# Attention: four of twelve turns of the probabilities go from TensorE to GpSimd and transposing transfers, and stand elsewhere in the written order

## The chip, the cores and the metric

The kernel runs on one core of one Trainium2 chip. The metric is the device time of one execution in microseconds (us). Before the change three runs took 966.99, 967.45 and 968.06 us; the median is 967.45 us. The profile is one further execution.

## What is computed

A trunk of two layers over 256 positions with 1024 features, all in float32: a gated linear recurrence, then attention, each between two half-step SwiGLU blocks. The change touches only the attention, which the reference computes for two query blocks of 128 positions:

```python
q = (xq @ w_q).reshape(Bn, S, N_HEADS, HEAD_DIM).transpose(0, 2, 1, 3) * (HEAD_DIM ** -0.5)
for blk in range(S // Q_BLOCK):
    q0 = blk * Q_BLOCK
    end = q0 + Q_BLOCK
    logits = jnp.einsum('bhqd,bhkd->bhqk', q[:, :, q0:end], k[:, :, :end]).astype(jnp.float32)
    logits = logits + c[:, :, q0:end, None] - c[:, :, None, :end]
    ...
    p = jax.nn.softmax(logits, axis=-1).astype(v.dtype)
    outs.append(jnp.einsum('bhqk,bhkd->bhqd', p, v[:, :, :end]))
o = jnp.concatenate(outs, axis=2).transpose(0, 2, 1, 3).reshape(Bn, S, D_ATTN)
return o @ w_o
```

There are 16 heads of 64 features. The first query block (the first half, `t == 0`) sees 128 keys, the second (`t == 1`) 256.

## The kernel before, in words

Every large product is made of three passes over split operands: a weight tile `raw` (512 KB, loaded by a transfer on SP's queue) is split into an upper part `whi` (ScalarE, L173) and a lower part `wlo` (VectorE, L177, which subtracts one SBUF tensor from another), and activations are split likewise (`xhi` and `xlo`, or `oh` and `ol` behind the attention). TensorE then runs upper by upper, upper by lower and lower by upper into one bank. Five `raw` buffers and nine pairs of parts stand between the loads and TensorE.

In the attention a group is four heads of the first half (groups 0 to 3) or two of the second (groups 0 to 7), that is 128 by 512 probabilities each. Four steps make a group:

- `logits` (l): TensorE multiplies queries and keys for two groups at once into two `gt` banks (L1138). VectorE adds the bias row by row and finds the maximum (L1147: `gt` in PSUM, bias in SBUF), adds and subtracts `cq` in two tiny tensor_tensor operations on `mx` (L1151, L1152; 128 by 4 or by 2 elements, all in SBUF), and ScalarE takes the exponentials and their sums (L1154).
- `norm` (n): VectorE inverts the sums (L1160) and multiplies the group by them (L1161, both inputs in SBUF).
- `turn` (t): TensorE transposes the group in four pieces of 128 by 128 into a `tr` bank (L1167), and ScalarE copies it to a `pT` tile (L1169).
- `values` (v): TensorE multiplies `pT` and the values (L1181). Behind two groups of the first half, or four of the second, ScalarE and VectorE split the result into `oh` and `ol` (L1187, L1188).

TensorE's program order is written out by hand. In the attention it is the string `ATT_ORDER`: a digit is half a weight unit (eight units of the query projection, L428 to L432, then eight of the output projection, L183 to L185, each once for either half of the positions), and a letter with a digit is the next step of that kind and that half. A letter l for an odd group does nothing, since the even one before it made both. Heads of the queries are turned two ticks after their projection is done (L1001, from a tile `htok` that VectorE writes at L996). The other engines' instructions, and the transfers, are put in order by the framework from priorities and due times, and then stand fixed in each engine's queue. Each queue runs in order.

The feed-forward blocks already turn their hidden activations without TensorE: GpSimd copies the tile into two planes of 16-bit halves (L527), SP issues a transposing transfer of the planes (L535), and GpSimd joins the halves again (L540). The keys take the same way through the helpers `planes`, `swap` and `join` (L212, L216, L220, or L1016).

Of the kernel before, what the change touches and what calls it, by code (L numbers as in the profile page):

```python
# [9 lines left out]
F32 = mybir.dt.float32  # L10
F32R = mybir.dt.float32r
BF16 = mybir.dt.bfloat16
U16 = mybir.dt.uint16
# [4 lines left out]
P = 128  # L18
# [25 lines left out]
def trunk_kernel(ctx: ExitStack, tc: tile.TileContext, A: dict, out: bass.AP):  # L44
# [6 lines left out]
    hpool = ctx.enter_context(tc.tile_pool(name="h", bufs=1))  # L51
# [6 lines left out]
    def nm(s):  # L58
        uid[0] += 1
        return f"{s}_{uid[0]}"  # L60
# [7 lines left out]
    def trbank():  # L68
        return psum.tile([P, 512], F32, tag="tr", name=nm("tr"), bufs=2)
# [36 lines left out]
    h = [hpool.tile([P, D], F32, tag=f"h{t}", name=f"h{t}") for t in range(2)]  # L106
# [103 lines left out]
    def planes(dst, src):  # L210

        nc.gpsimd.tensor_copy(dst.rearrange("p (h f) -> p h f", h=2), src.bitcast(U16).rearrange("p (f h) -> p h f", h=2))  # L212

    def swap(turned, halves):

        tc.keep_in_program_order(nc.sync.dma_start(turned.rearrange("p (a b) -> p a b", b=P), halves, transpose=True))  # L216

    def join(dst, turned):

        nc.gpsimd.tensor_copy(dst, turned.rearrange("p (h f) -> p h f", h=2))  # L220
# [895 lines left out]
    def attention(t):  # L1116

        ap = pools["a"]
# [4 lines left out]
        box = {}  # L1123
# [37 lines left out]
            nc.vector.tensor_tensor(pe, pe, sm.unsqueeze(2).to_broadcast([P, per, nk * P]), ALU.mult)  # L1161

        def turn(hg):
            tp = trbank()
            pev = box["pe", hg].rearrange("p a b -> p (a b)")
            for j in range(4):
                nc.tensor.transpose(tp[:, j * P:(j + 1) * P], pev[:, j * P:(j + 1) * P], ident)  # L1167
            pT = box["pT", hg] = ap.tile([P, 4, P], F32, tag="pT", name=nm("pT"), bufs=4)
            nc.scalar.activation(pT.rearrange("p a b -> p (a b)"), tp, AF.Copy)  # L1169

        def values(hg):

            hds = range(hg * per, (hg + 1) * per)
            if hds[0] % 8 == 0:
                box["po"] = mmbank()
            po, pT = box["po"].rearrange("p (a b) -> p a b", a=4), box["pT", hg]
            for j in range(0, per, 2):
                for k in range(nk):
                    for s in range(2):
                        hd = hds[j + s]  # L1180
                        nc.tensor.matmul(po[s * HD:(s + 1) * HD, hd % 8 // 2, :], kv["v"][k][:, hd * HD:(hd + 1) * HD],  # L1181
                                         pT[:, (j + s) * nk + k, :], start=k == 0, stop=k == nk - 1)
            if hds[-1] % 8 == 7:
                b = hds[-1] // 8
                oh_v = att["oh"][t][:, 4 * b:4 * b + 4, :].rearrange("p a b -> p (a b)")
                ol_v = att["ol"][t][:, 4 * b:4 * b + 4, :].rearrange("p a b -> p (a b)")
                nc.scalar.activation(oh_v, box["po"], AF.Copy)  # L1187
                nc.vector.tensor_tensor(ol_v, box["po"], oh_v.bitcast(F32), ALU.subtract)  # L1188

        return {c: [lambda i=i, f=f: f(i) for i in range(G)] for c, f in zip("lntv", (logits, norm, turn, values))}  # L1190

    def post_q(n):
        return lambda t, ps: heads_T(ps, t, n, HD ** -0.5, att["q"][t])

    for n in range(2):
# [9 lines left out]
    ffn_items(lambda: pools["f"], A["ffn2_w_gate"][1], A["ffn2_w_up"][1], A["ffn2_w_down"][1], A["ffn2_post_g"][1],  # L1205
              lambda t: None, last=True)

    ATT_ORDER = ("0 0 0 0 0 0 0 l0 0 1 n0 l0 1 1 t0 n0 1 l0 v0 1 t0 n0 l0 1 v0 n0 1 t0 l1 1 v0 t0 n1 l1 0 v0 "
                 "n1 l1 t1 0 n1 l1 t1 0 n1 l1 v1 v1 t1 0 n1 l1 t1 0 n1 l1 v1 v1 t1 0 n1 l1 t1 0 n1 v1 v1 0 t1 1 "
                 "t1 v1 1 v1 1 1 1 1 1 1")  # L1210


    def half(t, i):
# [178 lines left out]
    att_rows()  # L1392

    steps = [attention(0), attention(1)]
    nxt = [n_ffn3, n_ffn3]
    for c in ATT_ORDER.split():
        if c[0] in "lntv":
# [45 lines left out]
```

## Time and profile before

| | before |
|---|---|
| median of three runs | 967.45 us |
| the profiled execution | 967.64 us |
| its span in the trace | 965.9 us, so 1.7 us lie around it |
| TensorE busy | 957.7 us of the span |
| granted TensorE clock over the span | 0.998 |
| attention steps on TensorE | from 721.18 us (first logits) to 769.1 us (start of the last values) |

The chain of waits follows the work that ended last backwards from the end; it names the engine that sets the time. The list of waits says for how long an engine stood idle and what ended that. The timeline shows single instructions with their start and duration. Matmuls are pipelined, so that their durations overlap: what one costs is the distance from its start to the next start. A busy share close to one says little here; the absence of idle time in front of TensorE's instructions says more.

### The profile page before, as it was taken

The numbers are of one execution on the slowest core, as the hardware profiler recorded it, in microseconds if no ns is written. First come the engines' busy times: TensorE is split into PE (matmuls) and PEld (weight loads), VectorE is DVE, ScalarE is ACT, GpSimd is POOL, SyncE is SP. The second block draws the span as 40 slices with busy tenths as digits, with TensorE's granted clock in tenths as the row PEclk, the third lists the DMA queues.
The fourth block names the chain that finished last, engine by engine and source line by source line (L and its number), as shares of the span: only waits on it lengthen the run. The fifth ranks groups of instructions, "written<-read, shape, count | busy, mean of one in ns | idle before, by whom it ended". The sixth has DMA issues, their size and how long they took to land.

```text
span 965.9 us, 12879 instructions
## 1 busy us (share of the span) xinstructions
PE 957.7 (99%) x4591; PEld 793.3 (82%) x4591; DVE 637.2 (66%) x845; ACT 528.9 (55%) x753; POOL 207.1 (21%) x211
## 2 busy tenths in 40 slices
PE   9999999999999999999999999999999999999997
PEld 6888888898888888888898888888887788888885
DVE  6758764668998656664686566665487876666642
ACT  7447553568886555443565455444367855444431
POOL 2712330100001323230003632234020012232200
PEclk9999999999999999999999999999999999999999
DMA  8788996565337787776558879778772468777731
GB/s 283 226 229 251 260 283 196 157 198 156 120 108 234 205 236 214 202 245 195 134 179 279 243 233 260 225 216 263 227 256 71 134 200 233 209 224 235 216 109 44
DMA packets 144710, 197.74 MB, mean 205 GB/s; under 512 B 62942, under 2 KB 81734, under 8 KB 144518
## 3 DMA queue, kind: packets, MB, share of 16 engines
q1 hardware_dynamic: 141958, 190.01, 66.6%
q0 software_dynamic: 2080, 6.38, 2.0%
q8 instruction: 36, 0.59, 0.3%
q10 hardware_dynamic: 608, 0.53, 0.2%
q14 instruction: 28, 0.23, 0.1%
HBM read 182.19 MB, written 3.16 MB: 192 GB/s over the span
## 4 chain that ended last, share of the span: by engine, by line
PE 96%; DVE 1%; issue 1%; ACT 1%; POOLq 0%; POOL 0%; DVEq 0%; ACTq 0%
PE mm L428 16%; PE mm L429 16%; PE mm L432 16%; PE mm L183 13%; PE mm L185 13%; PE mm L184 13%; PE gt L779 2%; PE mm L1278 1%; PE mm L190 1%; PE mm L191 1%; PE mm L192 1%; PE gt L226 1%; PE tr L127 0%; ACT pe L1154 0%; PE mm L1181 0%
## 5 line engine op out<-in xcount | busy, mean ns | idle before, releaser
L177 DVE TENSOR_TENSOR wlo<-raw,whi 128x1024 fp32r<-128x1024 f32 (+5 forms) x329 | 415.8, 1270 | 231.6 <-ACT whi L173 229.5
L173 ACT ACTIVATE whi<-raw 128x1024 fp32r<-128x1024 f32 (+5 forms) x329 | 341.8, 1046 | 306.0 <-PE mm L432 126.3
L428 PE MATMUL mm<-whi,xhi 128*128 128x512 f32 x656 | 256.6, 391 | 0.0
L429 PE MATMUL mm<-wlo,xhi 128*128 128x512 f32 x656 | 255.5, 389 | 0.0
L432 PE MATMUL mm<-whi,xlo 128*128 128x512 f32 x656 | 202.1, 389 | 0.0
L428 PEld LDWEIGHTS mm<-whi,xhi 128*128 128x128 f32 x656 | 123.2, 188 | 25.9 <-issue 0.7
L432 PEld LDWEIGHTS mm<-whi,xlo 128*128 128x128 f32 x656 | 123.1, 188 | 25.8 <-DVE xlo L240 0.2
L429 PEld LDWEIGHTS mm<-wlo,xhi 128*128 128x128 f32 x656 | 123.2, 188 | 25.3 <-DVE wlo L177 0.3
L183 PE MATMUL mm<-whi,hhi 128*128 128x512 f32 x352 | 137.2, 390 | 0.0
L185 PE MATMUL mm<-whi,hlo 128*128 128x512 f32 x352 | 137.0, 389 | 0.0
L184 PE MATMUL mm<-wlo,hhi 128*128 128x512 f32 x352 | 136.9, 389 | 0.0
L540 POOL COPY pl<-prod 128x1024 uint16<-128x1024 uint16 (+1 forms) x48 | 68.5, 1427 | 169.9 <-DMA prod<-pl 169.9
L527 POOL COPY pl<-prod 128x1024 uint16<-128x1024 uint16 (+1 forms) x48 | 68.2, 1421 | 153.7 <-DVE prod L524 93.9
L198 POOL TENSOR_SCALAR nv<-ss 128x1 f32<-128x1 f32 x22 | 9.6, 437 | 318.0 <-ACT junk L205 318.0
L183 PEld LDWEIGHTS mm<-whi,hhi 128*128 128x128 f32 x352 | 66.1, 188 | 13.7
L185 PEld LDWEIGHTS mm<-whi,hlo 128*128 128x128 f32 x352 | 66.1, 188 | 13.7
L184 PEld LDWEIGHTS mm<-wlo,hhi 128*128 128x128 f32 x352 | 66.1, 188 | 13.5
L524 DVE SCALAR_TENSOR_TENSOR prod<-mm,rstd,sil 128x512 f32<-128x512 f32 (+1 forms) x48 | 33.7, 703 | 30.5 <-PE mm L432 24.4
L515 ACT ACTIVATE sil<-mm,rstd 128x512 f32<-128x512 f32 (+1 forms) x48 | 31.0, 648 | 33.2 <-PE mm L432 25.3
L546 DVE TENSOR_TENSOR hlo<-pl,hhi 128x512 fp32r<-128x512 f32 (+1 forms) x48 | 40.8, 849 | 4.3 <-ACT hhi L545 4.3
L183 PE MATMUL mm<-whi,xhi 128*128 128x512 f32 (+1 forms) x112 | 42.8, 382 | 0.0
L185 PE MATMUL mm<-whi,xlo 128*128 128x512 f32 (+1 forms) x112 | 42.5, 379 | 0.0
(217 smaller groups left out, 1047.7 us busy)
## 6 DMA issues: line engine op xcount, KB each, us to landing
raw<-in_ffn_w_down_dram SPq DMA_DIRECT2D x88, 512.0 KB
raw<-in_ffn_w_up_dram SPq DMA_DIRECT2D x80, 512.0 KB
raw<-in_ffn_w_gate_dram SPq DMA_DIRECT2D x78, 512.0 KB
raw<-in_rg_w_in_dram SPq DMA_DIRECT2D x10, 504.0 KB
raw<-in_rg_w_out_dram SPq DMA_DIRECT2D x10, 504.0 KB
raw<-in_ffn_w_gate_dram SPq DMA_DIRECT2D x19, 256.0 KB
raw<-in_ffn_w_up_dram SPq DMA_DIRECT2D x16, 256.0 KB
raw<-in_rg_w_in_dram SPq DMA_DIRECT2D x8, 512.0 KB
```

Of the source, the lines that this page charges most:

```text
L173: up = nc.scalar.activation(hi[:parts, c:c + m], rawv[:, c:c + m], AF.Copy)
L177: nc.vector.tensor_tensor(lo[:parts, c:c + m], rawv[:, c:c + m], hi[:parts, c:c + m].bitcast(F32), ALU.subtract)
L183: nc.tensor.matmul(ps, xh, wh, start=first, stop=False)
L184: nc.tensor.matmul(ps, xh, wl, start=False, stop=False)
L185: nc.tensor.matmul(ps, xl, wh, start=False, stop=last)
L428: nc.tensor.matmul(ps, get_x(t, k)[0], u.hi[:, c], start=k == 0, stop=False)
L429: nc.tensor.matmul(ps, get_x(t, k)[0], u.lo[:, c], start=False, stop=False)
L432: nc.tensor.matmul(ps, get_x(t, k)[1], u.hi[:, c], start=False, stop=k == nk - 1)
L524: nc.vector.scalar_tensor_tensor(pr[:, :nn], ps, rs[t][:, 0:1], s, ALU.mult, ALU.mult)
L527: nc.gpsimd.tensor_copy(halves.rearrange("p (h f) -> p h f", h=2), pr[:, :nn].bitcast(U16).rearrange("p (f h) -> p h f", h=2))
L540: nc.gpsimd.tensor_copy(halves.rearrange("p (f h) -> p h f", h=2), turned.rearrange("p (h a) b -> p h (a b)", h=2))
L546: keep(nc.vector.tensor_tensor(lv, x, hv.bitcast(F32), ALU.subtract))
```

## The change

For the first half, `turn` no longer uses TensorE and ScalarE. It goes through `turn_by_transfer`: GpSimd copies the group into planes (a tile `pl` with the tag `t1`, of which there are two buffers), SP issues a transposing transfer into a tile `turned` (with the tag `pT`, four buffers, shared with `htok` and the second half's `pT`), and GpSimd joins the planes back into `pl`, which `values` reads. The string that orders TensorE is written anew: `v0` stands later behind its `t0`, and the second half's `l1` and `n1` stand earlier against the products around them.

```diff
         def turn(hg):
+            if t == 0:
+                turn_by_transfer(hg)
+                return
             tp = trbank()
...
+        def turn_by_transfer(hg):
+
+            flat = box["pe", hg].rearrange("p a b -> p (a b)")
+            pT = hpool.tile([P, 512], F32, tag="t1", name=nm("pl"), bufs=2)
+            turned = ap.tile([P, 4, P], F32, tag="pT", name=nm("turned"), bufs=4).rearrange("p a b -> p (a b)").bitcast(U16)
+            planes(pT.bitcast(U16), flat)
+            swap(turned, pT.bitcast(U16))
+            join(pT.bitcast(U16).rearrange("p (f h) -> p h f", h=2), turned)
+            box["pT", hg] = pT.rearrange("p (a b) -> p a b", a=4)
...
-    ATT_ORDER = ("0 0 0 0 0 0 0 l0 0 1 n0 l0 1 1 t0 n0 1 l0 v0 1 t0 n0 l0 1 v0 n0 1 t0 l1 1 v0 t0 n1 l1 0 v0 "
-                 "n1 l1 t1 0 n1 l1 t1 0 n1 l1 v1 v1 t1 0 n1 l1 t1 0 n1 l1 v1 v1 t1 0 n1 l1 t1 0 n1 v1 v1 0 t1 1 "
-                 "t1 v1 1 v1 1 1 1 1 1 1")
+    ATT_ORDER = ("0 0 0 0 0 0 0 l0 0 1 n0 t0 l0 1 1 n0 t0 1 l0 1 l0 1 v0 1 n0 t0 l1 v0 1 n0 t0 n1 l1 0 n1 l1 t1 0 n1 l1 t1 v0 "
+                 "0 v0 n1 l1 v1 v1 t1 0 n1 l1 t1 0 n1 l1 v1 v1 t1 0 n1 l1 t1 0 n1 v1 v1 0 t1 1 t1 v1 1 v1 1 1 1 1 1 1 "
+                 "")
```

The helpers that it calls stand in the program already:

```python
    def planes(dst, src):
        nc.gpsimd.tensor_copy(dst.rearrange("p (h f) -> p h f", h=2), src.bitcast(U16).rearrange("p (f h) -> p h f", h=2))

    def swap(turned, halves):
        tc.keep_in_program_order(nc.sync.dma_start(turned.rearrange("p (a b) -> p a b", b=P), halves, transpose=True))

    def join(dst, turned):
        nc.gpsimd.tensor_copy(dst, turned.rearrange("p (h f) -> p h f", h=2))
```

Line numbers behind `turn` rise by 13 in the changed kernel, and those in the rest of `turn` by 3.

How the rows move is shown at three places. The first is TensorE where the output projection begins (`oh` and `ol` are the parts of the attention's output). Before, from the first half unit of that projection to the first turn of the second half:

```order
L183 MATMUL mm_6671<-whi_6336,oh_6347 128x512
L184 MATMUL mm_6671<-wlo_6337,oh_6347 128x512
L185 MATMUL mm_6671<-whi_6336,ol_6349 128x512
L183 MATMUL mm_6672<-whi_6336,oh_6347 128x512
L184 MATMUL mm_6672<-wlo_6337,oh_6347 128x512
L185 MATMUL mm_6672<-whi_6336,ol_6349 128x512
L1181 MATMUL mm_6657<-pT_6667,v_2938 64x128 x4
L1138 MATMUL gt_6687<-kT,qT_6345 128x256
L1138 MATMUL gt_6688<-kT,qT_6345 128x256
L1138 MATMUL gt_6687<-kT,qT_6345 128x256
L1138 MATMUL gt_6688<-kT,qT_6345 128x256
L1167 MATMUL tr_6709<-ident,pe_6634 128x128 x4
```

And after, from the same half unit to the same turn:

```order
L183 MATMUL mm_6658<-whi_6336,oh_6347 128x512
L184 MATMUL mm_6658<-wlo_6337,oh_6347 128x512
L185 MATMUL mm_6658<-whi_6336,ol_6349 128x512
L183 MATMUL mm_6659<-whi_6336,oh_6347 128x512
L184 MATMUL mm_6659<-wlo_6337,oh_6347 128x512
L185 MATMUL mm_6659<-whi_6336,ol_6349 128x512
L1138 MATMUL gt_6668<-kT,qT_6345 128x256
L1138 MATMUL gt_6669<-kT,qT_6345 128x256
L1138 MATMUL gt_6668<-kT,qT_6345 128x256
L1138 MATMUL gt_6669<-kT,qT_6345 128x256
L1170 MATMUL tr_6690<-ident,pe_6620 128x128 x4
```

The half unit and the turn are the same; the values between them are gone from there. What moved ahead of the piece: before, two half units, two turns, logits and values stood between the values from which `oh_6347` and `ol_6349` come and this half unit that reads them; now one half unit of the query projection stands there. The first pair of logits of the second half stood ahead by a half unit, values and a turn, and now stands ahead by values and a half unit.

The second place is VectorE at the same point, from the subtraction for a weight unit on. Before (`pe_6549` and `pe_6561` are groups 2 and 3 of the first half, `pe_6634` is group 0 of the second, and the operation of L1147 that writes `pe` is shown as ISA):

```order
L177 TENSOR_TENSOR wlo_6517<-raw_6514,whi_6516 128x1024
L1151 TENSOR_TENSOR mx_6560<-mx_6560,cq_2942 128x4
L1152 TENSOR_TENSOR mx_6560<-mx_6560,cq_2942 128x4
L1160 RECIPROCAL sm_6547<-sm_6547 128x4
L1161 TENSOR_TENSOR pe_6549<-pe_6549,sm_6547 128x512
L1188 TENSOR_TENSOR ol_6349<-mm_6572,oh_6347 128x512
L1160 RECIPROCAL sm_6547<-sm_6547 128x4
L1161 TENSOR_TENSOR pe_6561<-pe_6561,sm_6547 128x512
L1147 ISA pe_6634,mx_6633<-gt_6626,bias_6346 128x256
L1147 ISA mx_6633 128x1
```

And after, from the second inversion on (here `pe_6564` is group 3 of the first half, `pe_6620` and `pe_6628` are groups 0 and 1 of the second, and L1201 is the L1188 of before):

```order
L1160 RECIPROCAL sm_6550<-sm_6550 128x4
L1147 ISA pe_6620,mx_6619<-gt_6612,bias_6346 128x256
L1147 ISA mx_6619 128x1
L1161 TENSOR_TENSOR pe_6564<-pe_6564,sm_6550 128x512
L1147 ISA pe_6620,mx_6619<-gt_6613,bias_6346 128x256
L1147 ISA mx_6619 128x1
L1147 ISA pe_6628,mx_6627<-gt_6612,bias_6346 128x256
L1147 ISA mx_6627 128x1
L1201 TENSOR_TENSOR ol_6349<-mm_6594,oh_6347 128x512
L996 TENSOR_SCALAR htok_6647<-mm_6575,rstd_6395 128x512
L1151 TENSOR_TENSOR mx_6619<-mx_6619,cq_2943 128x2
```

Up to the first inversion and multiplication the rows are the same in both programs. Behind them, the lower part `ol` stood ahead of the first maximum over a row of the second half; now it and the `htok` of the second half's last query heads stand among those maxima, ahead of the small operations on `mx`.

The third place is SP's queue and GpSimd's. On SP, from the sixth load of the output projection's weights on, the changed program has

```order
L164 DMA raw_6735<-in_attn_w_o_dram 128x1024
L216 DMA_TRANSPOSE turned_6489<-pl_6488 128x8x128
L216 DMA_TRANSPOSE turned_6528<-pl_6527 128x8x128
L164 DMA raw_6794<-in_attn_w_o_dram 128x1024
L164 DMA raw_6815<-in_attn_w_o_dram 128x1024
L161 DMA raw_6868<-in_ffn_w_gate_dram 128x2x512
L216 DMA_TRANSPOSE turned_6608<-pl_6607 128x8x128
L216 DMA_TRANSPOSE turned_6652<-pl_6651 128x8x128
```

where the program before has the four loads alone, in the same order. On GpSimd all eight copies are new, and stand in a row between the norms of two residual steps:

```order
L212 COPY pl_6488<-pe_6442 128x1024
L212 COPY pl_6527<-pe_6454 128x1024
L220 COPY pl_6488<-turned_6489 128x2x512
L220 COPY pl_6527<-turned_6528 128x2x512
L212 COPY pl_6607<-pe_6552 128x1024
L212 COPY pl_6651<-pe_6564 128x1024
L220 COPY pl_6607<-turned_6608 128x2x512
L220 COPY pl_6651<-turned_6652 128x2x512
```

Each copy of L212 waits for `norm` of its group, each transfer for its copy, and each join for its transfer; the third and fourth copies also wait until TensorE has read the first and second `pl`, since there are two buffers.

## The prediction, made before the result was known

> **What bounds the kernel now.** I read the page first, for the engine that sets the end.
>
> ```profile
> PE 957.7 (99%) x4591; PEld 793.3 (82%) x4591; DVE 637.2 (66%) x845; ACT 528.9 (55%) x753; POOL 207.1 (21%) x211
> ...
> PE 96%; DVE 1%; issue 1%; ACT 1%; POOLq 0%; POOL 0%; DVEq 0%; ACTq 0%
> ```
>
> The chain that ended last is 96% TensorE. The list of waits with TensorE alone says whether it ever stands still:
>
> ```profile
> PE tr L127 <- PEq L1428: 0.8, 1, 0.8
> PE gt L779 <- issue: 0.5, 1, 0.5
> ```
>
> Two waits in the whole execution, neither in the attention. So work taken from TensorE shortens the end one for one, and every new wait of TensorE lengthens it one for one. VectorE, ScalarE and GpSimd count only where they make TensorE wait.
>
> **What TensorE saves.** Its timeline in the attention (start, duration) gives a price for each block, as the distance from its start to the next start:
>
> ```profile
> 722.28 0.50 PE L428 MATMUL mm<-whi,xhi 128*128 128x512 f32 x1
> ...
> 723.77 0.39 PE L428 MATMUL mm<-whi,xhi 128*128 128x512 f32 x1
> ...
> 725.13 0.39 PE L428 MATMUL mm<-whi,xhi 128*128 128x512 f32 x1
> ...
> 728.31 0.60 PE L1167 MATMUL tr<-ident,pe 128*128 128x128 f32 x4
> 728.67 0.47 PE L428 MATMUL mm<-whi,xhi 128*128 128x512 f32 x1
> 728.98 0.39 PE L429 MATMUL mm<-wlo,xhi 128*128 128x512 f32 x1
> 729.20 0.39 PE L428 MATMUL mm<-whi,xhi 128*128 128x512 f32 x1
> ...
> 735.23 0.60 PE L1001 MATMUL tr<-ident,htok 128*128 128x128 f32 x4
> 735.76 0.66 PE L1181 MATMUL mm<-pT,v 128*64 128x128 f32 x8
> 736.35 0.50 PE L428 MATMUL mm<-whi,xhi 128*128 128x512 f32 x1
> ...
> 738.37 1.13 PE L1138 MATMUL gt<-kT,qT 64*128 64x256 f32 x8
> 739.43 0.50 PE L428 MATMUL mm<-whi,xhi 128*128 128x512 f32 x1
> ...
> 742.02 0.48 PE L183 MATMUL mm<-whi,oh 128*128 128x512 f32 x1
> ...
> 742.56 0.39 PE L185 MATMUL mm<-whi,ol 128*128 128x512 f32 x1
> ...
> 749.47 1.13 PE L1138 MATMUL gt<-kT,qT 64*128 64x256 f32 x8
> ```
>
> A turn takes 0.36 us to the next start (728.31 to 728.67), and the first product behind it 0.31 instead of 0.22, so one group costs 0.36 + 0.08 = 0.44. Four groups go: **-1.7 us**, nothing beside them, as TensorE never waits. The four copies on ScalarE go too and save nothing, since it is no bound. All else that TensorE does only changes place.
>
> From 728.31 on, the changed order is: half unit, logits, two half units, query turn, values, half unit, logits, values, half unit, first half unit of the output projection. A half unit takes 1.36 (723.77 to 725.13), or 1.49 behind another kind; a query turn 0.53; values 0.59; logits 1.06, and about 0.1 for each change of kind. Without waits TensorE reaches the first values at 734.3, the second values at 737.5, the product with `ol` (third row of the first output half unit) at 740.05, the next logits at 741.1, the second half's first turn at 742.15, and the third logits of the second half at 749.47 - 1.7 = 747.8.
>
> **What the new path costs.** GpSimd copies, the transfer lands, GpSimd joins. The trace has the same steps in the next block, with VectorE beside them:
>
> ```profile
> 818.61 1.90 POOL L527 COPY pl<-prod 128x1024 uint16<-128x1024 uint16 x1 [3.86 <-DVE prod L524]
> 823.70 1.68 POOL L540 COPY pl<-prod 128x1024 uint16<-128x1024 uint16 x1 [3.19 <-DMA prod<-pl]
> 828.12 1.04 POOL L527 COPY pl<-prod 128x1024 uint16<-128x1024 uint16 x1 [2.74 <-DVE prod L524]
> ```
>
> ```profile
> 818.39 1.22 DVE L177 TENSOR_TENSOR wlo<-raw,whi 128x1024 fp32r<-128x1024 f32 x1
> ...
> 828.38 1.86 DVE L177 TENSOR_TENSOR wlo<-raw,whi 128x1024 fp32r<-128x1024 f32 x1 [0.39 <-ACT whi L173]
> ```
>
> From the end of the planes (820.51) to the join are 3.2 us. A GpSimd copy takes 1.04 alone. Where VectorE's subtraction starts first (818.39), the copy ends 0.9 behind it and lasts 1.90; where the copy starts first (828.12), the subtraction lasts 1.86 instead of 1.22 and ends 1.08 behind the copy. So the two exclude each other: whoever is later waits.
>
> [...]
>
> Now VectorE and ScalarE, whose order is fixed:
>
> ```profile
> 726.72 0.69 DVE L1161 TENSOR_TENSOR pe<-pe,sm 128x512 f32<-128x512 f32 x1
> 728.74 0.69 DVE L1161 TENSOR_TENSOR pe<-pe,sm 128x512 f32<-128x512 f32 x1
> 729.48 1.22 DVE L177 TENSOR_TENSOR wlo<-raw,whi 128x1024 fp32r<-128x1024 f32 x1
> ...
> 731.28 1.21 DVE L177 TENSOR_TENSOR wlo<-raw,whi 128x1024 fp32r<-128x1024 f32 x1
> ...
> 734.25 1.22 DVE L177 TENSOR_TENSOR wlo<-raw,whi 128x1024 fp32r<-128x1024 f32 x1
> ...
> 738.63 0.18 DVE L1160 RECIPROCAL sm<-sm 128x4 f32<-128x4 f32 x1 [0.84 <-ACT pe L1154]
> ...
> 742.49 0.17 DVE L1160 RECIPROCAL sm<-sm 128x2 f32<-128x2 f32 x1 [0.49 <-ACT pe L1154]
> ...
> 758.43 0.69 DVE L1161 TENSOR_TENSOR pe<-pe,sm 128x512 f32<-128x512 f32 x1
> 759.04 0.42 DVE L1147 CUSTOM_DVE_ANT_0 pe<-gt,bias 128x256 f32<-128x256 f32 x1
> ...
> 759.38 0.69 DVE L1188 TENSOR_TENSOR ol<-mm,oh 128x512 fp32r<-128x512 f32 x1
> ```
>
> ```profile
> 736.96 0.39 ACT L1154 ACTIVATE pe<-pe,mx 128x128 f32<-128x128 f32 x1
> ...
> 741.36 0.51 ACT L1154 ACTIVATE pe<-pe,mx 128x256 f32<-128x256 f32 x1 [2.29 <-DVE mx L1152]
> ```
>
> 1. Group 0 is normed at 727.4, its planes are made by 728.6, and its join can start at 731.8. Group 1 is normed at 729.4; its planes wait for the subtraction of 729.48 and end at 731.5; the one of 731.28 then ends at 732.55. The first join runs behind that, to 733.8. The first values want it at 734.3: **no wait**, 0.5 to spare.
> 2. The tiny additions on `mx` (L1151) read two SBUF tensors too; I take it that they also wait for a copy. Then the first costs 0.25, the third subtraction starts at 734.55 instead of 734.25, and the second join (ready at 731.5 + 3.2 = 734.7) gets its turn at 735.75 and ends at 737.0: 0.5 before the second values.
> 3. Behind that join stand group 3's `mx`, so that its exponentials start at 737.4. From there to the inversion are 1.7 (736.96 to 738.63): 739.1. In the new order this inversion has maxima, the norm of group 3 and then `ol` behind it: 0.4 + 0.61 + 0.35 + 0.35 = 1.7 further on, 740.8 to 741.5. TensorE wanted `ol` at 740.05: **+1.45**.
> 4. `ol`, `htok` and a maximum put the second half's first `mx` at 742.5; exponentials from 742.7, inversion 1.1 later (741.36 to 742.49). But the third join becomes ready at 742.5 as well (group 2 normed at 738.2, planes to 739.3, 3.2 more) and holds up the `mx` pair that stands ahead of the inversion until 743.9; inversion 744.2, a maximum, norm 744.6 to 745.3. TensorE, late by 1.45, wants to turn at 742.15 + 1.45 = 743.6: **+1.75**.
>
> Behind that turn I find no further wait: the third and fourth values come after 747, their joins end by about 747, and the third logits read queries that ScalarE has copied before. The two transfers of groups 2 and 3 stand on SP's queue behind a weight load and ahead of the next; before, no load is issued between 735.49 and 752.69, so the loads have room. On GpSimd nothing but the eight copies is queued there. VectorE's maxima of the second half write the `pe` buffers that the planes read (there are three), and ScalarE's second-half `pT` shares four buffers with the transfers' targets; by the times above the planes end a microsecond ahead of such a maximum (739.3 against 740.4) and the third join ahead of such a copy, so neither adds to the sum. The rows of SP's queue:
>
> ```profile
> 735.49 0.38 SPq L161 DMA_DIRECT2D raw<-in_ffn_w_gate_dram  x1
> 752.69 3.88 SPq L161 DMA_DIRECT2D raw<-in_ffn_w_gate_dram  x3
> ```
>
> **Sum:** -1.7 + 1.45 + 1.75 = +1.5 us on the profiled execution's 967.64 us (span 965.9 and 1.7 around it), which lies 0.2 above the median of the runs: **969.1 us**.
>
> The weak point is step 2, since no row has a tiny addition beside a copy: its bounds are no wait at all and a whole copy each, 1.35 us (the 1.68 of 823.70 is a join that had to wait first). I take the whole wait, as for the large ones. [...]
>
> **The rivals.**
> - *Only large operations wait* (for: only those are seen waiting). Then group 3's exponentials start at 736.0, `ol` is late by 0.55 and the turn by 1.4, since `ol`, `htok` and three norms still stand in its way: -1.7 + 1.95 = +0.25, 967.9 us. Without any waiting between the engines it is 967.4.
> - *Slower: the third join comes first.* In step 4 the last `mx` and the join are ready within 0.1 us of each other. If the join gets in first, the exponentials start only after it: 1.1 more, 970.2 us. It decides at 742.5, and any slip of VectorE by 0.1 brings it about.
> - *The transfers take longer*, 5.2 us as when one follows another closely (planes to 540.36, join 545.58):
>
> ```profile
> 536.37 3.99 POOL L212 COPY pl<-ktok 128x1024 uint16<-128x1024 uint16 x2
> ...
> 545.58 1.35 POOL L1016 COPY kT<-ktok 128x1024 uint16<-128x1024 uint16 x1 [2.56 <-DMA ktok<-pl]
> ```
>
>   The first join then ends at 735.1, the first values wait 0.9, and the joins fall on later norms: about 971 us. Against: nothing else is being moved at 728.6.
> - *The whole saving comes through*, 967.64 - 1.7 = 965.9 us. It needs VectorE 1.4 us earlier than I find at the turn.
>
> **How the numbers follow.** The forecast has 0.42, the join first 0.25, only large ones 0.20, slow transfers 0.07, the whole saving 0.06. About 0.2% (1.9 us) is what a measurement of this kernel can tell from no change. Slower by more, above 969.4 us: the second and fourth case and a quarter of the forecast's spread of half a microsecond, 0.42. Faster by more, below 965.5: half of the last, 0.03. Within: 0.55. The range leaves out the whole saving and the worst of the slow transfers: 967.0 to 971.2 us.
>
> **What would show it.** TensorE should have two new waits, one before the third product of the first output half unit (on `ol`) and one before the second half's first turn, together 3.2 us, and none before the values. Tiny `mx` operations of a microsecond and more beside a GpSimd copy would bear step 2 out; 0.15 us beside one would refute it. Values that wait for a join would show that the path is longer than 3.2 us. No new wait at all would make the prediction wrong.

## The result, and the profile after

Six runs of the changed kernel took 969.83 to 971.36 us, median 970.12; six of the kernel before beside them have a median of 967.23. The ratio is 1.0029, with a 95% interval of 1.0019 to 1.0039: the change made the kernel **slower by 2.9 us**, or 0.29%. The forecast was 969.1 us within 967.0 to 971.2. The range held the time, but the likeliest class, no change within 0.2%, did not come about.

The profiled execution took 970.27 us with a span of 968.6. From its page, the busy times, and the shares of the chain that ended last:

```profile
PE 956.8 (99%) x4575; PEld 792.6 (82%) x4575; DVE 645.1 (67%) x845; ACT 527.5 (54%) x749; POOL 217.2 (22%) x219
...
PE 96%; DVE 2%; issue 1%; ACT 1%; DMA 0%; POOLq 0%; POOL 0%; DVEq 0%; ACTq 0%
```

TensorE has lost its 16 pieces of four turns (4591 matmuls before, 4575 now) and 0.9 us of busy time. GpSimd has eight copies more and 10 us, VectorE 8 us more with the same 845 instructions: some of them last longer. The list of waits, TensorE's alone (total, times, longest):

```profile
PE tr L1170 <- DVE sm L1160: 2.8, 1, 2.8
PE mm L185 <- DVE ol L1201: 1.2, 1, 1.2
```

These two are new in the attention, and they are the two places that the prediction named. (A third new one, 0.3 us for a small load, L134, lies at the start of the kernel.) TensorE's timeline shows where they stand:

```profile
733.96 0.66 PE L1194 MATMUL mm<-pl,v 128*64 128x128 f32 x8
...
737.20 0.66 PE L1194 MATMUL mm<-pl,v 128*64 128x128 f32 x8
...
739.52 0.40 PE L184 MATMUL mm<-wlo,oh 128*128 128x512 f32 x1
741.08 0.50 PE L185 MATMUL mm<-whi,ol 128*128 128x512 f32 x1 [1.17 <-DVE ol L1201]
...
742.21 1.13 PE L1138 MATMUL gt<-kT,qT 64*128 64x256 f32 x8
746.10 0.93 PE L1170 MATMUL tr<-ident,pe 128*128 128x128 f32 x4 [2.76 <-DVE sm L1160]
...
747.25 0.63 PE L184 MATMUL mm<-wlo,oh 128*128 128x512 f32 x1
747.68 0.63 PE L185 MATMUL mm<-whi,ol 128*128 128x512 f32 x1
...
753.27 1.14 PE L1138 MATMUL gt<-kT,qT 64*128 64x256 f32 x8
```

Neither of the first two values (733.96, 737.20) waits. The product with `ol` waits for 1.17 us, the second half's first turn for 2.76. What the list of waits does not show is behind that turn: the products start 0.43 us apart (747.25 to 747.68), where such products stood 0.22 to 0.24 apart before. The busy time by stretches of two microseconds, with the granted clock in the third column from the end, says why:

```profile
744.00:746.00 2.00, 0.00 (x0) 0.00 (x0) 1.51 (x6) 1.44 (x6) 1.33 (x1) 1.00 0.00 0
746.00:748.00 2.00, 1.90 (x7) 1.74 (x8) 1.94 (x11) 0.93 (x2) 0.00 (x0) 0.57 0.00 0
748.00:750.00 2.00, 2.00 (x9) 1.51 (x9) 1.12 (x4) 0.76 (x4) 0.00 (x0) 0.57 0.00 0
750.00:752.00 2.00, 2.00 (x18) 1.53 (x17) 0.00 (x0) 1.82 (x5) 0.00 (x0) 1.00 0.00 0
```

TensorE does nothing in the first stretch, and in the next two it runs at a granted clock of 0.57, with at most half as many matmuls as in the fourth. These figures are means of two microseconds: from 746.3 to 749.7 us the clock of this trace is 0.50 throughout. Behind the first wait, of 1.17 us, the clock stays at 1.00 (the stretches from 740 to 744).

VectorE's timeline shows what made the turn late:

```profile
735.34 1.24 DVE L1151 TENSOR_TENSOR mx<-mx,cq 128x4 f32<-128x4 f32 x1
736.62 0.16 DVE L1152 TENSOR_TENSOR mx<-mx,cq 128x4 f32<-128x4 f32 x1
...
740.34 0.69 DVE L1201 TENSOR_TENSOR ol<-mm,oh 128x512 fp32r<-128x512 f32 x1
...
742.02 1.25 DVE L1152 TENSOR_TENSOR mx<-mx,cq 128x2 f32<-128x2 f32 x1
...
744.49 0.17 DVE L1160 RECIPROCAL sm<-sm 128x2 f32<-128x2 f32 x1 [0.95 <-ACT pe L1154]
...
744.96 1.00 DVE L1161 TENSOR_TENSOR pe<-pe,sm 128x512 f32<-128x512 f32 x1
```

And GpSimd's, from the first join on:

```profile
731.53 2.08 POOL L220 COPY pl<-turned 128x1024 uint16<-128x1024 uint16 x1 [0.21 <-DMA turned<-pl]
734.54 2.08 POOL L220 COPY pl<-turned 128x1024 uint16<-128x1024 uint16 x1 [0.93 <-DMA turned<-pl]
...
741.98 1.33 POOL L220 COPY pl<-turned 128x1024 uint16<-128x1024 uint16 x1 [1.04 <-DMA turned<-pl]
744.14 1.33 POOL L220 COPY pl<-turned 128x1024 uint16<-128x1024 uint16 x1 [0.82 <-DMA turned<-pl]
```

Each long row of VectorE lies in a join. A tiny addition of 128 by 4 elements lasts 1.24 us and ends 0.04 before the join that began at 734.54; its fellow behind that lasts 0.16. The one of 742.02 comes 0.04 us behind the start of the third join and lasts 1.25. The norm of 744.96 meets the fourth join and lasts 1.00 instead of 0.69.

**The sum.** TensorE's last product starts at 962.10 us, before at 958.74. Of these 3.36 us, -0.28 arose ahead of the attention (its first logits start at 720.90, before at 721.18), so that 3.64 arose from there on. The terms are -1.71 for the turns, 1.17 and 2.76 for the waits, and about 1.6 for the slow products (measured below), together 3.8. The way there is less smooth than that. At the second half's third logits (753.27, before 749.47) the kernel is 4.08 behind, counted from the first logits. The waits account for that if they are counted by starts and not as idle time: the product with `ol` starts 1.33 late (741.08 instead of 739.52 + 0.23), the turn 2.83 (746.10 instead of 742.21 + 1.06), and with these the sum is 4.0. Up to the last product 0.44 is regained.

**The end.** The span grew only by 2.7, since what lies behind the start of the last product takes 6.5 us here and 7.2 in the profiled execution before. In the profiled executions of this study that goes with the kernel: 6.4 to 6.6 us in all ten with transfers for these turns, 7.2 in all three without. So 0.5 to 0.7 us of the time of each kernel with transfers is won behind TensorE's last product, and not in the attention. What wins it was not followed up.

### The profile page after: what moved, and what is told of

It reads as the page before. It is cut to its first block, busy times and chain, and to the rows that moved or that the text cites. A ratio compares the mean times of both kernels' runs of the same rounds, so it can differ in the third digit from the quotient of the medians.

```text
span 968.6 us, 12871 instructions
## 1 busy us (share of the span) xinstructions
PE 956.8 (99%) x4575; PEld 792.6 (82%) x4575; DVE 645.1 (67%) x845; ACT 527.5 (54%) x749; POOL 217.2 (22%) x219
## 4 chain that ended last, share of the span: by engine, by line
PE 96%; DVE 2%; issue 1%; ACT 1%; DMA 0%; POOLq 0%; POOL 0%; DVEq 0%; ACTq 0%
PE mm L428 16%; PE mm L432 16%; PE mm L429 16%; PE mm L183 13%; PE mm L185 13%; PE mm L184 13%; PE gt L779 2%; PE mm L1291 1%; PE mm L190 1%; PE mm L191 1%; PE mm L192 1%; PE gt L226 1%; ACT pe L1154 1%; PE mm L1194 1%; PE tr L1170 0%
## 5 line engine op out<-in xcount | busy, mean ns | idle before, releaser
L177 DVE TENSOR_TENSOR wlo<-raw,whi 128x1024 fp32r<-128x1024 f32 (+5 forms) x329 | 421.3, 1287 | 230.4 <-ACT whi L173 228.9
L184 PE MATMUL mm<-wlo,xhi 128*128 128x512 f32 (+1 forms) x112 | 42.3, 378 | 0.0
```

Source lines behind the costliest of these rows:

```text
L177: nc.vector.tensor_tensor(lo[:parts, c:c + m], rawv[:, c:c + m], hi[:parts, c:c + m].bitcast(F32), ALU.subtract)
L184: nc.tensor.matmul(ps, xh, wl, start=False, stop=False)
```

## The experiments

**Theory A**, the prediction's with the clock added: a VectorE instruction with two SBUF tensors in, however small, waits for a GpSimd copy; such waits make `ol` and the second half's first turn late; TensorE's long wait then lets the granted clock fall. **Rivals**: the new order costs the time by itself; the transfers or copies cost it in another way than through what is late; or the slow products come from traffic beside them and not from the idle time. All runs are compared with runs of the kernel before on the same chip, with medians of 967.26 to 967.39 us.

### Filling the idle time

In the first run ten products of constants stand ahead of the second half's first turn. They add 2.36 us of work that nobody needs.

```diff
-... 1 n0 t0 n1 l1 0 n1 l1 t1 0 ...
+... 1 n0 t0 n1 l1 0 n1 l1 k10 t1 0 ...
-        if c[0] in "lntv":
+        if c[0] == "k":
+            keep_busy(int(c[1:]))
+        elif c[0] in "lntv":
```

> The changed kernel with ten products of constants (128 by 512, bf16, result never read) put on TensorE right ahead of the second half's first turn, where it waits 2.8 us. Theory A (VectorE makes TensorE wait, and the granted clock falls behind the long wait): the wait shrinks to about 0.6 us, the products behind the turn keep their distance of 0.23 us instead of 0.43, and the time falls by about 1.5 us to 968.6, although work was added. Rival B (the products behind the turn are slow because of the transfers or copies beside them, not because TensorE stood still): they stay slow and the time stays at 970.1 or above.

Measured: 969.63 us, ratio 1.0023 (1.0014 to 1.0033), no slower than the changed kernel in spite of the added work. TensorE's timeline at the wait, and the stretch behind it:

```profile
743.34 2.36 PE L127 MATMUL tr<-const-bfloat16-1.0 128*128 128x512 bf16 x10
746.15 0.63 PE L1170 MATMUL tr<-ident,pe 128*128 128x128 f32 x4 [0.45 <-DVE sm L1160]
```

```profile
746.00:748.00 2.00, 1.85 (x11) 1.58 (x11) 1.59 (x9) 0.63 (x3) 0.00 (x0) 1.00 0.00 0
```

The turn starts at 746.15, practically as in the changed kernel, the clock is 1.00 in every stretch of two microseconds from 740 to 752, and the products behind the turn stand 0.23 apart (746.85 to 747.08). So the slow products come from the idle time. The 968.6 that were expected did not come about: the second half's second turn now waits for 0.40 on a copy of ScalarE, so that the third logits follow the first turn by 6.20 us (752.35 - 746.15) instead of 7.17 in the changed kernel, and the 0.44 that the changed kernel regains further on is not regained here. A second run fills only 0.95 us of the wait and leaves 1.8:

> The changed kernel with 4 instead of 10 constant products ahead of the second half's first turn: 0.95 us of the wait of 2.76 are filled, and 1.8 are left. It asks how long an idle time the granted clock bears. If 1.8 us are too long, the clock falls to about 0.57 behind the turn as in the changed kernel, and the time stays at 969.8 to 970.5 us; if not, the products behind the turn run at full pace as with 10 of them, and it is 969.1 to 969.8, about 0.5 below the changed kernel.

Measured: 968.64 us, ratio 1.0015 (1.0006 to 1.0024), below both ranges of the expectation. The profiled execution took 971.07, since it was behind by some 2 us ahead of the attention already, so only distances within it are read. Its busy time by stretches, from the turn (which starts at 748.44) on:

```profile
746.00:748.00 2.00, 0.68 (x4) 0.10 (x1) 1.15 (x4) 1.80 (x8) 1.33 (x1) 1.00 0.00 0
748.00:750.00 2.00, 1.56 (x9) 1.41 (x10) 2.00 (x10) 0.71 (x2) 0.00 (x0) 1.00 0.00 0
750.00:752.00 2.00, 2.00 (x19) 1.53 (x19) 1.31 (x6) 2.00 (x7) 0.00 (x0) 1.00 0.00 0
```

And TensorE's timeline, the turn and the next logits:

```profile
748.44 0.63 PE L1170 MATMUL tr<-ident,pe 128*128 128x128 f32 x4 [1.76 <-DVE sm L1160]
...
754.03 1.13 PE L1138 MATMUL gt<-kT,qT 64*128 64x256 f32 x8
```

An idle time of 1.76 us leaves the clock at 1.00 here. From the turn to the next logits are 5.59 us (754.03 - 748.44), in the changed kernel 7.17 (753.27 - 746.10), with the same work between them. **The fallen clock costs 1.58 us**, and that is the term which the prediction lacks. Here all of it reaches the end: from the first logits to the last product this kernel takes 2.05 us more than the kernel before, the changed one 3.64. In the changed kernel 2.76 us without a matmul were enough for a fall to 0.50, from 746.3 to 749.7, or for 3.4 us.

### The order and the transfers apart

The order of the changed kernel with all turns on TensorE (the first half's `t0` set where the turned tiles are needed):

```diff
-            if t == 0:
-                turn_by_transfer(hg)
-                return
...
-... l0 0 1 n0 t0 l0 1 1 n0 t0 1 l0 1 l0 1 v0 1 n0 t0 l1 v0 1 n0 t0 n1 l1 0 n1 l1 t1 0 n1 l1 t1 v0 0 v0 ...
+... l0 0 1 n0 l0 1 1 n0 t0 1 l0 1 t0 l0 1 v0 1 n0 l1 v0 1 t0 n0 n1 l1 0 t0 n1 l1 t1 0 n1 l1 t1 v0 0 v0 ...
```

> The order alone: all turns on TensorE as before, in the changed kernel's order; only the first half's turns are set back, to where their results are needed next. No copy and no transfer is added. Theory A: the tiny additions on mx take 0.15 us again, the waits on ol and before the second half's first turn fall under 0.5 and 1 us, no clock falls; 967 to 968.3 us. Rival C (the order is what costs): waits of about 1.2 and 2.8 us stay, and with all turns back on TensorE the time is about 970 to 972.

Measured: 967.3 us, ratio 0.9999 (0.999 to 1.0008), and no wait of TensorE but the two that the kernel before has. The order costs nothing that shows in the time (0.2 us by the trace, from the first logits to the last product). The transfers with the order of before:

> The transfers alone: the changed kernel with the old written order, where the values stand close behind their turn. Theory A: the first values, wanted at about 731 us, wait 2.5 to 3 us for a join that ends at about 733.6, the third and fourth about 1 us each, so -1.7 + 4.7 = +3 us or 970.3, up to 972 if the clock falls behind a wait. Rival C (the new order is what costs, the transfers are hidden): no such wait on joins over 0.5 us, about 966 to 967.

Measured: 972.26 us, ratio 1.0054 (1.0041 to 1.0067), at the upper end of what was expected. Its waits, and the granted clock behind the first of them:

```profile
PE mm L1194 <- POOL pl L220: 5.4, 3, 3.0
```

```profile
730.00:732.00 2.00, 0.23 (x5) 0.04 (x2) 2.00 (x4) 0.64 (x1) 1.79 (x2) 1.00 0.21 38
732.00:734.00 2.00, 0.78 (x9) 0.61 (x10) 2.00 (x19) 0.55 (x3) 1.17 (x1) 1.00 1.05 172
734.00:736.00 2.00, 2.00 (x7) 1.61 (x7) 2.00 (x2) 1.11 (x6) 1.87 (x1) 0.72 0.89 330
736.00:738.00 2.00, 2.00 (x6) 1.52 (x5) 0.94 (x4) 0.00 (x0) 1.07 (x2) 0.50 1.00 390
738.00:740.00 2.00, 2.00 (x16) 1.36 (x16) 0.00 (x0) 1.10 (x3) 0.14 (x1) 0.93 1.00 95
```

Here the values wait for their joins, and the clock falls behind a wait of 3.0 us once more. The new order with its later places of `v0` thus spares the changed kernel these 5.4 us. Since that order alone costs nothing, the changed kernel's own loss comes from what the transfers do in it.

### The turn one half unit later

If the turn is merely asked for too early, then a half unit moved ahead of it covers the wait:

```diff
-... n1 l1 0 n1 l1 t1 0 n1 l1 t1 v0 0 v0 n1 ...
+... n1 l1 0 n1 l1 0 t1 0 n1 l1 t1 v0 v0 n1 ...
```

> The changed kernel with one half unit of the output projection moved ahead of the second half's first turn (taken from between the third and fourth values). Theory A: TensorE comes to the turn about 1.5 us later, waits about 1.3 us instead of 2.8, and the clock does not fall: 970.1 - 1.5 - 1.5 = 967.1 us, within 0.7 of it. Rival B (slow products come from the transfers or copies beside them): 968.6. Rival D (the loss is in the transfers' own queue): 970.

Measured: 967.18 us, ratio 1.0001 (0.9992 to 1.001). Its waits:

```profile
PE mm L185 <- DVE ol L1201: 1.2, 1, 1.2
...
PE tr L1170 <- DVE sm L1160: 0.7, 1, 0.7
```

One half unit, moved by one place, gives back the whole loss, 2.9 us: 2.0 of waiting (0.75 is left of 2.76), and the clock, whose mean in the profiled execution is 0.999 (0.996 in the changed kernel). Nothing of the transfers was touched. By the trace TensorE's last product still comes 0.6 later than in the kernel before, and the shorter end makes up for that.

### What makes VectorE late

In these runs the two tiny additions become one instruction for each head, with the shift as a scalar operand, so that a single SBUF tensor goes in:

```diff
-                nc.vector.tensor_tensor(nm_q[:, :per], mx[:, :per], cq, ALU.add)
-                nc.vector.tensor_tensor(nm_q[:, :per], nm_q[:, :per], cq, ALU.subtract)
+                for j in range(per):
+                    nc.vector.tensor_scalar(nm_q[:, j:j + 1], mx[:, j:j + 1], cq[:, j:j + 1], cq[:, j:j + 1],
+                                            ALU.add, ALU.subtract)
```

> The changed kernel, with the two tiny additions on mx (L1151, L1152: two SBUF tensors in) written once for each head with the shift as a scalar operand held in SBUF, so that only one SBUF tensor goes in. Theory A (a VectorE instruction with two SBUF tensors in, however small, waits for a GpSimd copy, and these two waits push the product with ol and the second half's first turn back): the new small instructions last 0.1 to 0.2 us each also beside a join, TensorE's wait for ol falls from 1.17 to below 0.5, its wait at the turn from 2.76 to below 1.5, the granted clock does not fall behind it, and the time is 966.0 to 968.0 us, 0.2 to 0.4% below the changed kernel. Rival (any small VectorE instruction that reads SBUF waits for a copy, or the waits come from the norms' large products alone): instructions of 1 us and more stay beside the joins, ol and the turn wait as before, 969 to 970.5 us. In between, at about 968.5: the waits come half from the tiny additions and half from the product of the norm (L1161, 1.00 instead of 0.69).

Measured: 966.61 us, ratio 0.9991 (0.9982 to 1.0). TensorE's waits for `ol` and at the turn are gone; it waits for 0.48 on `htok`, 0.52 on the second join and 0.19 at the logits. A control has the same instructions with the subtrahend as a second SBUF tensor:

```diff
-                    nc.vector.tensor_scalar(nm_q[:, j:j + 1], mx[:, j:j + 1], cq[:, j:j + 1], cq[:, j:j + 1],
-                                            ALU.add, ALU.subtract)
+                    nc.vector.scalar_tensor_tensor(nm_q[:, j:j + 1], mx[:, j:j + 1], cq[:, j:j + 1], cq[:, j:j + 1],
+                                                   ALU.add, ALU.subtract)
```

> The control for the run with scalar operands (966.61 us): the same number of small instructions on mx, one for each head and with the same scalar operand, but the subtrahend comes in as a second SBUF tensor. The order on VectorE and GpSimd differs in places from that run's, because the scheduler prices the two forms differently, so the time alone proves little; the single instructions do. Theory A: one or more of these 128x1 instructions that meet a GpSimd copy last 0.7 us and more (the one with a single SBUF tensor lasted 0.2 beside copies), what stands behind them is late, and TensorE waits for 1 us or more in all in the attention: 967.0 to 969.5 us. Rival (the number and order of the instructions did it, not the second input): every one lasts 0.2 to 0.3 us, 966.3 to 967.0.

Measured: 967.11 us, ratio 0.9996 (0.9987 to 1.0005), with waits of 1.26 for `ol` and 0.29 at a turn. The times of the two runs cannot decide, the single instructions can. The group of these in the run with one SBUF tensor, from 724 to 748 us (shortest, median and longest in ns, then the first and last start):

```profile
L1152 DVE TENSOR_SCALAR mx<-mx,cq x21: 259/265/273, 724.3 to 746.5; 128x1 f32<-128x1 f32 x21
```

The same in the control:

```profile
L1152 DVE SCALAR_TENSOR_TENSOR mx<-mx,cq x20: 191/210/1070, 725.0 to 745.4; 128x1 f32<-128x1 f32 x20
```

All 21 with one tensor take the same 0.26 to 0.27 us. That is more than the 0.1 to 0.2 that were expected, but no more beside a copy than elsewhere, and four of them stand beside one nearly all the time. VectorE's row and GpSimd's:

```profile
735.49 0.82 DVE L1152 TENSOR_SCALAR mx<-mx,cq 128x1 f32<-128x1 f32 x4
```

```profile
735.52 1.04 POOL L212 COPY pl<-pe 128x1024 uint16<-128x1024 uint16 x1 [1.70 <-DVE pe L1162]
```

With two tensors, one element for each partition can take 1.07 us. VectorE's rows in the control and GpSimd's:

```profile
743.79 1.07 DVE L1152 SCALAR_TENSOR_TENSOR mx<-mx,cq 128x1 f32<-128x1 f32 x1
...
745.38 0.99 DVE L1152 SCALAR_TENSOR_TENSOR mx<-mx,cq 128x1 f32<-128x1 f32 x1
```

```profile
743.57 1.33 POOL L220 COPY pl<-turned 128x1024 uint16<-128x1024 uint16 x1 [3.22 <-DMA turned<-pl]
744.81 1.55 POOL L212 COPY pl<-pe 128x1024 uint16<-128x1024 uint16 x1
```

Each of the two ends when the copy beside it ends, at 744.9 and 746.4. This bears out what the prediction took for its weak point, for the waits of the instructions. For the time it is less clear-cut: the framework orders VectorE and GpSimd differently in these two programs (in the run with one tensor, the first join stands ahead of the second planes; in the control, the third join ahead of the fourth planes), and the intervals of the two runs overlap. How much of the gain belongs to the operands and how much to the order stays open.

> The kernel before, with the two tiny additions written with scalar operands as in the other two runs and nothing else changed: the control for them. TensorE does not wait in the attention of the kernel before, so all theories expect 967.0 to 967.8 us, no difference from the kernel before. A gain or a loss of 0.5 us or more here would have to be taken off from the other two.

Measured, for the kernel before with scalar operands: 967.26 us, ratio 0.9999 (0.999 to 1.0007). In the kernel without the copies the form is worth nothing.

### Fewer transfers, and both remedies

Transfers for the first two groups alone (`if t == 0 and hg < 2`); groups 2 and 3 are turned on TensorE, where the run with the order alone has their turns:

> Transfers for the first two groups of the first half alone, whose joins end before the second half's norms begin; groups 2 and 3 are turned on TensorE, and the order of the list is that of the run with the new order and all turns on TensorE, but for the first two. Theory A: two turns are saved (0.9 us), the tiny additions beside the second join are late by about 1.1 but the third join, which came in ahead of the last of them, is gone, so the second half's first turn waits for 1.0 us or less, ol for 0.5 to 1.2, and the clock does not fall: 966.5 to 968.0 us. Rival (the cost is in the transfers or the copies themselves, each one of four adding a share): half of the loss of the changed kernel, 968.5 to 969.2.

Measured: 967.48 us, ratio 1.0002 (0.9993 to 1.0011). Its waits:

```profile
PE mm L185 <- DVE ol L1201: 0.6, 1, 0.6
...
PE tr L1170 <- DVE pe L1161: 0.3, 1, 0.3
```

By these rows two turns save 0.9 us and the two waits take it back; by the trace the last product comes 0.8 later, and the shorter end makes up for most of that. A cost of each transfer by itself would have left 968.5 and more.

Scalar operands and the later turn together:

> The one with scalar operands in L1151 and L1152, and with the second half's first turn one half unit later, as in the run that moved only the turn (967.18 us). Theory A: with the tiny waits gone and the turn later, TensorE does not wait in the attention at all (both waits below 0.3 us), and the whole saving of four turns, 1.7 us, is left: 965.5 to 966.8 us, ratio to the kernel before 0.998 to 0.9994. Rival: the saving is not there even without waits, because the products beside the transfers or the copies are slower by something the waits do not show: 967.0 to 967.7.

Measured: 966.47 us, ratio 0.999 (0.9982 to 0.9999), the lowest median of all kernels here, but not clear of the run with scalar operands alone (966.61). The expectation that TensorE would not wait was wrong:

```profile
PE mm L1195 <- POOL pl L220: 0.6, 1, 0.6
PE tr L1001 <- DVE htok L996: 0.5, 1, 0.5
...
PE gt L1138 <- DVE mx L1147: 0.2, 1, 0.2
```

These 1.3 us of the 1.7 saved are still lost. By the trace the last product comes only 0.1 us earlier, counted from the first logits, than in the kernel before; most of the 0.9 that was measured is the shorter end. With the second values one half unit later as well:

```diff
-... n0 t0 l1 v0 1 n0 t0 n1 l1 0 ...
+... n0 t0 l1 1 v0 n0 t0 n1 l1 0 ...
```

> The run with scalar operands and the turn later (966.47 us), with the second group's values one half unit later too, since they waited for their join for 0.59. Theory A (the copies cost only through what is late): that wait goes, nothing new comes, and 965.5 to 966.3 us are left, nearly the whole saving. Rival: the product with ol, which needs these values, stands now directly behind them and waits for 0.5 to 1.5 us instead: 966.3 to 967.5.

Measured: 967.6 us, ratio 1.0009 (1.0001 to 1.0018). The rival held in place, its time being 0.1 above the range: the output projection needs these values, and now waits for both of its operands.

```profile
PE mm L183 <- ACT oh L1201: 1.3, 1, 1.3
PE mm L185 <- DVE ol L1202: 1.1, 1, 1.1
```

All runs beside the sum of what their profiles show. The sum is the turns saved, plus TensorE's new waits in the attention, the filling products and the fallen clock (1.58 in the changed kernel; in the run with the old order 1.7 by the clock of three stretches of 2 us, 2 × (0.28 + 0.50 + 0.07), a way that gives 1.7 for the changed kernel too). The two columns behind it are differences to the kernel before in the profiled executions: from the first logits to the start of TensorE's last product, and from there to the end of the span.

| run | sum, us | to the last product, us | behind it, us | measured against before, us (medians) |
|---|---|---|---|---|
| changed kernel | -1.7 + 1.2 + 2.8 + 1.6 = +3.8 | +3.6 | -0.7 | +2.9 |
| ten filling products | -1.7 + 1.2 + 0.45 + 0.4 + 2.4 = +2.7 | +3.2 | -0.7 | +2.2 |
| four filling products | -1.7 + 1.2 + 1.8 + 0.9 = +2.2 | +2.1 | -0.7 | +1.4 |
| transfers, old order | -1.7 + 5.4 + 1.7 = +5.4 | +5.4 | -0.7 | +4.9 |
| new order, turns on TensorE | 0 | +0.2 | 0.0 | -0.1 |
| turn later | -1.7 + 1.2 + 0.7 = +0.2 | +0.6 | -0.7 | -0.2 |
| scalar operands | -1.7 + 0.5 + 0.5 + 0.2 = -0.5 | -0.1 | -0.7 | -0.8 |
| kernel before, scalar operands | 0 | -0.1 | 0.0 | -0.1 |
| scalar operands, turn later | -1.7 + 0.5 + 0.6 + 0.2 = -0.4 | -0.1 | -0.6 | -0.9 |
| two SBUF tensors | -1.7 + 1.3 + 0.3 = -0.1 | +0.4 | -0.7 | -0.2 |
| two groups | -0.9 + 0.6 + 0.3 = 0.0 | +0.8 | -0.5 | +0.1 |
| scalar operands, turn and values later | -1.7 + 0.5 + 1.3 + 1.1 = +1.2 | +1.2 | -0.7 | +0.3 |

The large losses and the small differences come out as such. The two columns from the traces together lie within 0.4 us of every measurement, which speaks for a shorter end in the other executions too. Up to the last product the sums lie within 0.2 us of the trace for the changed kernel, four filling products, the old order and the values later; for the other runs with transfers they are 0.4 to 0.8 too low. A part of that is the way of counting, as with the two waits of the changed kernel above; the rest was not followed up. In the profiled executions no kernel saves more than 0.1 us on TensorE: most of what the fastest two gain in time lies behind its last product.

## Why the prediction was right or wrong

- **The turns, -1.7.** Right as far as it shows: 16 matmuls less, and without a wait TensorE reached the first values at 733.96, where 734.3 had been forecast, with an execution that was 0.28 ahead.
- **Step 1, no wait before the first values.** Right. The first join ended at 733.6 (731.53 + 2.08), forecast 733.8.
- **Step 2, the tiny additions wait too.** Right: 1.24 and 1.25 us beside a join in the changed kernel, 0.15 to 0.2 otherwise, and the control shows that the second SBUF tensor does it (up to 1.07 us with it, 0.26 to 0.27 with one tensor). The second join ended at 736.6, forecast 737.0.
- **Step 3, `ol` late by 1.45.** Right in place and cause. As a delay of the start, which is how the forecast counts, it was 1.33 (1.17 as idle time): VectorE's chain was about 0.4 earlier than forecast, and TensorE 0.3.
- **Step 4, the turn late by 1.75.** This step failed. It found the third join and the first group's `mx` ready at the same 742.5, let that pair go first and made only the next pair wait. In the trace the join starts at 741.98 and the second addition of the first pair 0.04 behind it, waits for the whole join, and the exponentials start only behind it. So the second rival's mechanism ("the third join comes first") took place. The turn was late by 2.83 (2.76 as idle time), 1.1 more than forecast, and that this is the rival's 1.1 is luck: since the chain was half a microsecond early, the inversion came only 0.3 later than forecast (744.49 against 744.2). Another 0.3 is the norm, which meets the fourth join and lasts 1.00 instead of 0.69; no step had priced that. TensorE came to the wait 0.3 earlier, and small distances make up the rest.
- **The granted clock.** No step had it. Behind 2.76 us of idle time the clock fell to 0.50, and the products behind it cost 1.58 more. Behind the 1.75 that was forecast it need not have fallen: the run with 1.76 us kept it at 1.00.
- **The end of the kernel.** No step had this either: 0.7 us less behind TensorE's last product.
- **The rivals.** "Only large ones wait" is refuted by the control, where 128 by 1 elements took 1.07 us beside a copy. "Slow transfers" did not come about: no values wait, and the joins begin as forecast. Of "the whole saving", 0.9 us came through at best in the time, with scalar operands and the turn later, and only 0.1 of that on TensorE.

The time of 970.1 is thus not the second rival's 970.2 for that rival's reasons alone: its mechanism took place, the clock came on top, and the regained 0.44 and the shorter end took some of it back. That the two numbers agree is luck, and so in part is it that the range held.

## What to carry to other kernels

Where TensorE never waits, price a saving on it by the first place where another engine becomes late, and in a tie between two engines of which one waits for the other (here an addition that lasted 1.25 us beside a join instead of 0.15) take the worse end. Look for instructions with two SBUF tensors on the path beside GpSimd copies, however small: here they took up to 1.25 us, and with a scalar operand in place of the second tensor 0.27 at most. Before a design is dropped for a wait of two or three microseconds, move one piece of independent work ahead of it; here that was worth 2.9 us, a part of it from the clock alone, which cost 1.58 in the changed kernel.

## What was not expected of the hardware

The granted clock fell to 0.50 behind one idle stretch of TensorE, of 2.76 us in the changed kernel and of 3.0 in the run with the old order, for 3.4 us each time: from 746.3 to 749.7, and from 734.9 to 738.3 (worked out from 0.72, 0.50 and 0.93 in its stretches of two microseconds), there 1.7 us behind the restart at 733.22. Behind 1.76 us (four filling products) or 1.17 (changed kernel) it stayed at 1.00 in the profiled executions. Filling products of constants, 0.95 us of them, were enough to prevent the fall.

The length of the idle time does not decide alone. At the end of a kernel TensorE has nothing more to do, and its clock fell there too. In the kernel before its last product ends at 959.13 us (958.74 + 0.39), and the clock is 1.00 until 962.3 and 0.50 from 962.4 on, some 3.2 us behind; in the changed kernel it ends at 962.49 (962.10 + 0.39), and the clock is 1.00 until 964.7 and 0.50 from 964.8 on, 2.2 us behind. In the attention the logits ahead of the idle stretch end at 743.34 (742.21 + 1.13) in the changed kernel, 3.0 us ahead of the fall, and at 730.23 (729.07 + 1.16) in the run with the old order, 4.7 ahead of it, with work again in the last 1.7. So 2.2 us without work were enough once, and 3.2 passed before the fall another time. The run with the values later too may belong here: its longest wait in the profiled execution is 1.3 us, but three of its eleven executions have a mean granted clock of 0.996 or 0.997 instead of 0.999, and take 969.35 to 970.83 us where the others take 967.42 to 967.98. Where the clock fell in those three is not known. How long a wait it takes, and how that depends on the moment at which it begins, was not tried.
